# A list scheduler's model of two vector engines that take turns, new prices for products, and a reservation for the SSD transposes

## The chip, the cores and the metric

The kernel runs on one core of a Trainium2 chip. The metric is the device time of one execution in microseconds; the times of three runs and one profiled execution of the kernel before are given below.

## What is computed

Two layers of an encoder over 768 tokens (a prompt of 256 and a sample of 512, same weights, laid side by side). Cut to what matters:

```python
def _layer(x, ...):
    h = _rmsnorm(x, norm1_w)
    proj = h @ w_in                        # 1024 -> all mixer inputs and three gates
    o_ssd = _ssd_branch(z, xbc, dt_raw, ...)   # conv over 5 taps, silu, chunked scan both ways, 4 groups
    o_gla = _gla_branch(gq, gk, gv, gog, ...)  # gated linear attention, chunks of 64, both ways
    o_att = _attn_branch(aq, ak, av, ...)      # qk-norm, rotary, softmax
    merged = g0 * (o_ssd @ w_br_ssd) + g1 * (o_gla @ w_br_gla) + g2 * (o_att @ w_br_attn)
    x = x + merged @ w_out
    gate, up = _split(_rmsnorm(x, norm2_w) @ w_ffn_in, ...)
    return x + (silu(gate) * up) @ w_ffn_out
```

Everything is float32. Large products are made from operands split into a high and a low part of type float32r, with three products (high high, high low, low high) for each; small products inside the mixers are float32 or float32r.

## The kernel before, in words

Features lie on the partitions and the 768 tokens along the free dimension. A large product of 128 output features (`gemm_a`) is 24 or 48 matmuls of 384 columns into one of two PSUM tiles `g`. Each 128x512 unit of weights is loaded by SyncE, split by ScalarE (high part) and by GpSimd or VectorE (low part, `wunit`, L605): by GpSimd from the start of a layer to the end of the SSD, by VectorE after it.

A builder records every operation on views of named buffers, in program order. In a layer the order is: the projections for attention and for the other mixers with attention's own work between them (`att_group`); GLA, two pairs of heads (`gla_pair`), and then the eight products `g2`/`ba` (`gate_branch`); the SSD, where each of four groups has four products `xbc` with convolutions and transposes (`ssd_inputs`), the chunked scan of the group (`ssd_group`, `ssd_state`), and then one, three, two and two of the eight products `g1`/`bg`; then `z`, `g0`/`bs`, the output projection and the FFN.

`Plan.schedule` (L438) turns this into a fixed order for each engine's queue. It is a list schedule over a model: each engine takes, whenever it is idle in the model, the earliest operation in program order whose inputs are there and whose buffers are free (weights' splits and the evacuations of large products come first, `first`). What the model believes an operation to take comes from `Plan.cost` (L355): for VectorE 70 ns plus 1.04 ns per element (60 more with a scalar operand), for GpSimd's `tensor_tensor` 150 ns plus 2.1 ns per element, for a float32r product n / 2.4 ns. In the model every engine runs by itself. The program that is emitted holds the order alone; on the chip each engine goes through its queue and waits for what it needs.

Buffers are taken when the first operation that touches them is scheduled (`take`, L519). The tags of PSUM's `g` are taken in program order, so the large products follow each other in program order whatever the prices are; what the model sets is where the mixers' small products stand between them. PSUM has two tiles `ma` and two `mb` for small products, taken by whoever comes first. In the SSD the arrays `xn` (256 features by tokens) and `bn` exist once, and belong to one group at a time. The transposes of a group (L1411) write PSUM tiles `ma`, and ScalarE copies these into `xn` or `bn` (L1414). `reserve` (L382) lets one operation take further buffers together with its own; before the change attention alone uses it.

Of the kernel before, what the change touches and what calls it, by code (L numbers as in the profile page):

```python
# [16 lines left out]
P = 128  # L17
# [61 lines left out]
# gate inputs (16 columns each) that go with the products of 256 columns  # L79
# [5 lines left out]
# ---------------------------------------------------------------------------  # L85
# Recording and scheduling.  The builder below records engine operations on
# views of named buffers; `Plan` then orders them (a list schedule over the
# engines' queues) and emits them in that order into Tile, which derives every
# wait.  Buffers of phase 0 have their place for the whole program; the rest of
# SBUF is cut into cells, of which each holds, per phase, one Tile tile with  # L90
# buffers of one kind (operands of float32r products, or anything else).
# ---------------------------------------------------------------------------
class View:
# [82 lines left out]
    def region(self):  # L176
        """(first, last + 1) over partitions and over the elements of one."""
        dims = self.dims
        p = (0, 1)
        lo = hi = self.off[1]  # L180
        if self.buf.space in "SP":
            n, s = dims[0]
            p = (self.off[0], self.off[0] + (n - 1) * s + 1)
            dims = dims[1:]
        for n, s in dims:
            if s >= 0:
                hi += (n - 1) * s
            else:
                lo += (n - 1) * s
        hi += 1  # L190
        if self.buf.space == "P":
            lo, hi, p = lo // 512 * 512, -(-hi // 512) * 512, (0, 128)
        return p[0], p[1], lo, hi
# [62 lines left out]
class Op:  # L256
    __slots__ = ("i", "eng", "fn", "args", "kw", "deps", "succ", "cost", "prio", "bufs", "wait", "ready", "end",
                 "table", "label")
# [13 lines left out]
class Plan:  # L272
# [25 lines left out]
    def record(self, eng, fn, args, kw):  # L298
# [49 lines left out]
        op.cost = self.cost(eng, fn, writes[0], reads) + extra + 120 * ("accum_out" in kw)  # L348
        for j in deps:
            self.ops[j].succ.append(op)  # L350
# [4 lines left out]
    def cost(eng, fn, out, reads):  # L355
        n = out.free()
        if eng == "tensor":
            if fn == "transpose":
                return 107
            if out.buf.space == "P" and reads[0].dtype == F32R:  # L360
                return 3 + (n / 2.4 if n >= 256 else 4 * n / 2.4)
            return 3 + (210 if n <= 64 else 4 * n / 2.4)
# [18 lines left out]
    @staticmethod  # L381
    def reserve(op, *views):  # L382
        """The buffers of the views are taken together with those of the operation."""
        for b in {v.buf for v in views} - set(op.bufs):
            op.bufs.append(b)
            b.users += 1

# [36 lines left out]
    def home(self, slot):  # L424
        """The Tile tile that the buffers of a slot live in."""
# [12 lines left out]
    def schedule(self):  # L438
# [5 lines left out]
        self.dma_free = 0.0  # L444
# [16 lines left out]
        while ev:  # L461
# [11 lines left out]
            while todo:  # L473
# [3 lines left out]
                while avail[e]:  # L477
# [12 lines left out]
                    if e == "sync":  # L490
                        start = max(now, self.dma_free)
                        self.dma_free = start + cost
                        idle_at[e] = now + 60
                        op.end = start + cost + 1900
                    else:
                        op.end = idle_at[e] = now + cost
# [68 lines left out]
class Pool:  # L565
    """Tags of one phase: the buffers of later phases take the place of earlier ones."""
# [8 lines left out]
class Builder:  # L575
# [12 lines left out]
    def first(self):  # L588
        """What feeds the tensor engine's products goes before the mixers' operations."""
# [79 lines left out]
    def sumsq(self, src, accs, last, eng=None, which=0):  # L669
        """Squares of one tile of features, added up on a vector engine; the last tile is left to the product."""  # L670
# [12 lines left out]
    def rstd(self, accs, nat, pool=None, ts=(0, NT)):  # L683
        """1 / rms of each token: nat with the tokens on partitions, and as rows over all partitions."""
# [88 lines left out]
    def layer(self, l):  # L773
# [161 lines left out]
    def finish(self, ps, xa, acc):  # L935
        """The last tile of features, and the final norm, by halves of the tokens."""
# [30 lines left out]
    def gate_inputs(self):  # L967
        """The inputs of the gates (SSD steps, GLA low rank), features on partitions."""
# [140 lines left out]
    def att_heads(self, t, i, span, nk, j, qT, kT, v2, oh, ol):  # L1109
        """Two heads of one tile of queries; their output goes to the rows of one tile of features."""  # L1110
# [81 lines left out]
    def gla_pair(self, p):  # L1192
# [10 lines left out]
        for d in range(2):  # L1203
# [12 lines left out]
            # scores within blocks of 64  # L1216
# [13 lines left out]
            # between the blocks, and with the state  # L1230
# [158 lines left out]
    def ssd_inputs(self, g):  # L1389
# [4 lines left out]
        for i in range(4):  # L1394
# [12 lines left out]
            if i < 3:  # L1407
                for a, b in ((0, 3), (3, 6)):
                    pt = self.pm.tile([P, 512], F32, tag="ma")
                    for t in range(a, b):  # L1410
                        self.pe.transpose(pt[:, (t - a) * P:(t - a + 1) * P], acc[:, self.toff(t)], self.ident)  # L1411
# [12 lines left out]
    def three(self, o, lhs, rhs):  # L1424
        """A product of split operands: hi hi, hi lo and lo hi."""
# [202 lines left out]
```

## Time and profile before

| | us |
|---|---|
| three runs | 3242.95, 3247.67, 3248.82 |
| median | 3247.67 |
| span of the profiled execution, first to last instruction | 3241.8 |
| TensorE busy in it | 3076.5 (95%) |
| VectorE busy | 1830.7 (56%) |
| ScalarE busy | 1304.3 (40%) |
| GpSimd busy | 1053.0 (32%) |
| mean granted TensorE clock, share of 2.4 GHz | 0.983 |

The profiled execution is known by its span; no time is recorded for what lies around it, and the median of the runs is 5.9 us above the span. Busy time of TensorE counts the whole flight of a matmul, and matmuls are pipelined, so a busy TensorE is not one at its peak. Every operation is emitted from one line (L554), so the line tells nothing; forms of operands and the stretch of time do. `base_P` is PSUM, `base_S` the buffers that keep their place for the whole program, `cell` those that change from phase to phase.

### The profile page before, as it was taken

What the parts mean: (1) busy time and instruction counts of PE and PEld (TensorE: products, weight loads), DVE (VectorE), ACT (ScalarE), POOL (GpSimd) and SP (SyncE); (2) the same over time, 40 slices, a digit from 0 to 9 for tenths busy, and PEclk for the clock granted to TensorE, in tenths of its full rate; (3) what the DMA queues carried; (4) which work ended last, traced back from release to release, by engine and by line L of the source; (5) the groups of instructions that cost most, each with busy time, mean ns of one, the idle gap of its engine ahead of it and who ended that gap; (6) DMA issues with size and microseconds to landing.
All of it is one profiled execution on the core that took longest, in us unless ns stands there. A gap on an engine that the chain in (4) does not pass through costs nothing.

```text
span 3241.8 us, 47503 instructions
## 1 busy us (share of the span) xinstructions
PE 3076.5 (95%) x18288; PEld 3003.9 (93%) x18288; DVE 1830.7 (56%) x3115; ACT 1304.3 (40%) x2285; POOL 1053.0 (32%) x1028
## 2 busy tenths in 40 slices
PE   8989988888999999999999899889899999999998
PEld 8989888878999999999999898788889999999998
DVE  4866888888523332333458568898884234333233
ACT  4756655444423221212356665454443232222123
POOL 5524656565232000000164255565642320000002
PEclk8999999999999999999999999999999999999999
DMA  3123223443334322222322232333333352222222
GB/s 115 59 70 111 73 73 96 108 108 100 101 87 128 117 66 62 62 66 62 97 69 62 69 114 69 90 92 95 108 114 95 87 174 67 62 65 62 62 62 69
DMA packets 191954, 279.49 MB, mean 86 GB/s; under 512 B 16688, under 2 KB 89776, under 8 KB 191728
## 3 DMA queue, kind: packets, MB, share of 16 engines
q1 hardware_dynamic: 191728, 276.46, 29.1%
q8 instruction: 144, 2.36, 0.3%
q14 instruction: 82, 0.67, 0.1%
HBM read 235.30 MB, written 41.09 MB: 85 GB/s over the span
## 4 chain that ended last, share of the span: by engine, by line
PE 75%; DVE 18%; ACT 2%; issue 2%; DMA 2%; POOL 1%; DVEq 0%; SPq 0%; POOLq 0%; ACTq 0%
PE base_P L554 75%; DVE cell L554 16%; DVE base_S L554 2%; ACT cell L554 1%; POOL cell L554 1%; DMA cell<-d_cs 1%; DMA d_ce<-cell 1%; ACT base_S L554 0%; ACT L554 0%; DMA cell<-d_ce 0%; POOL base_S L554 0%; DMA cell<-xT 0%; SPq L554 0%; DVEq L1623 0%; DVEq L554 0%
## 5 line engine op out<-in xcount | busy, mean ns | idle before, releaser
L554 PE MATMUL base_P<-base_S 128*128 128x384 f32 (+3 forms) x12452 | 2290.7, 336 | 10.0 <-DVE base_S L554 5.9
L554 PEld LDWEIGHTS base_P<-base_S 128*128 128x128 f32 x12452 | 2118.3, 191 | 18.5 <-DVE base_S L554 7.5
L554 ACT ACTIVATE base_S<-base_S 128x512 fp32r<-128x512 f32 (+6 forms) x830 | 550.0, 667 | 1242.3 <-PE base_P L554 889.0
L554 POOL TENSOR_TENSOR cell<-cell,base_S 128x512 f32<-128x512 f32 (+3 forms) x308 | 338.7, 1115 | 1387.4 <-ACT base_S L554 1289.3
L554 DVE TENSOR_TENSOR base_S<-base_S,base_S 128x512 fp32r<-128x512 f32 (+1 forms) x400 | 283.6, 709 | 680.9 <-issue 516.3
L554 PE MATMUL base_P<-cell,base_S 128*128 128x384 f32 x3136 | 574.5, 337 | 0.0
L554 PEld LDWEIGHTS base_P<-cell,base_S 128*128 128x128 f32 x3136 | 551.0, 188 | 0.0
L554 POOL TENSOR_TENSOR base_S<-base_S,base_S 128x512 fp32r<-128x512 f32 (+1 forms) x232 | 331.3, 1429 | 342.3 <-ACT base_S L554 186.6
L554 PE MATMUL base_P<-cell,cell 128*128 128x256 f32 (+3 forms) x1696 | 335.4, 316 | 104.6 <-DVE cell L554 85.8
L554 PEld LDWEIGHTS base_P<-cell,cell 128*128 128x128 f32 x1696 | 257.6, 196 | 145.6 <-DVE cell L554 90.5
L554 DVE TENSOR_TENSOR base_S<-base_P,base_S 128x768 f32<-128x768 f32 x228 | 217.6, 954 | 224.9 <-PE base_P L554 217.9
L554 DVE SCALAR_TENSOR_TENSOR cell<-cell,base_S,cell 128x128 f32<-128x128 f32 (+1 forms) x320 | 263.7, 858 | 30.5 <-ACT cell L554 27.5
L554 DVE TENSOR_TENSOR cell<-base_P,cell 128x256 f32<-128x256 f32 (+6 forms) x401 | 196.1, 496 | 144.9 <-PE base_P L554 117.2
L554 ACT ACTIVATE cell<-cell 128x256 fp32r<-128x256 f32 (+7 forms) x362 | 191.3, 545 | 179.8 <-DVE cell L554 146.6
L554 DVE TENSOR_TENSOR cell<-cell,cell 128x256 fp32r<-128x256 f32 (+7 forms) x282 | 217.6, 791 | 16.7 <-ACT cell L554 9.8
L554 ACT ACTIVATE cell<-base_P 128x256 f32<-128x256 f32 (+6 forms) x344 | 147.7, 439 | 188.9 <-PE base_P L554 182.4
L554 ACT ACT_TABLE_LOAD x147 | 188.6, 1283 | 29.3 <-DVE cell L554 21.6
L554 PE MATMUL base_P<-base_S,cell 128*128 128x128 f32 (+2 forms) x908 | 154.8, 278 | 30.4 <-DVE cell L554 16.6
L554 POOL TENSOR_TENSOR cell<-cell,cell 128x256 f32<-128x256 f32 (+6 forms) x196 | 134.3, 702 | 113.1 <-DVE cell L554 84.0
L554 PEld LDWEIGHTS base_P<-base_S,cell 128*128 128x128 f32 x908 | 112.9, 149 | 49.6 <-DVE cell L554 22.0
L554 DVE SCALAR_TENSOR_TENSOR cell<-cell,base_S 128x128 f32<-128x128 f32 x192 | 114.3, 646 | 8.1 <-POOL cell L554 6.5
L554 POOL TENSOR_TENSOR base_S<-base_S 128x768 f32<-128x768 f32 x32 | 66.5, 2077 | 96.5 <-DVE base_S L554 96.1
(57 smaller groups left out, 1147.4 us busy)
## 6 DMA issues: line engine op xcount, KB each, us to landing
base_S<-wts SPq DMA_DIRECT2D x584, 256.0 KB, 2.7
cell<-d_cs SPq DMA_DIRECT2D x96, 256.0 KB, 4.6
d_part<-base_S SPq DMA_DIRECT2D x32, 384.0 KB, 2.6
base_S<-d_part SPq DMA_DIRECT2D x32, 384.0 KB, 3.3
base_S<-wts SPq DMA_DIRECT2D x32, 272.0 KB, 2.7
d_y<-cell SPq DMA_DIRECT2D x48, 128.0 KB, 1.9
base_S<-d_y SPq DMA_DIRECT2D x16, 384.0 KB, 3.4
d_x<-base_S SPq DMA_DIRECT2D x16, 384.0 KB, 2.5
```

The source lines that it names most:

```text
L554: f(*[real(x) for x in op.args], **{k: real(x) for k, x in op.kw.items()})
```

## The change

Three edits; the rest of the diff takes comments out.

First, an operation gets a flag `port`: set for every operation of GpSimd, and for those of VectorE whose operands all lie in SBUF. In the model a flagged operation starts only when the flagged one scheduled before it has ended, so that the two engines take turns. Second, the prices of products: a float32r product of 384 columns goes from 163 to 175.3 ns, float32 ones are priced by the same 0.4486 ns per column, small ones at 222 ns. Third, the first of each three SSD transposes takes `xn` or `bn` together with its PSUM tile. No operation is added or removed; the emitted program has the same operations, and their order and the place of some buffers come out anew.

```diff
+        op.port = eng == "gpsimd" or eng == "vector" and all(v.buf.space == "S" for v in writes + reads)
...
-                return 3 + (n / 2.4 if n >= 256 else 4 * n / 2.4)
-            return 3 + (210 if n <= 64 else 4 * n / 2.4)
+                return 3 + (.4486 * n if n >= 256 else 4 * .4486 * n)
+            return 3 + (222 if n <= 128 else 4 * .4486 * n)
...
-        self.dma_free = 0.0
+        self.dma_free = port_free = 0.0
...
+                    elif op.port:
+                        op.end = idle_at[e] = port_free = max(now, port_free) + cost
                     else:
                         op.end = idle_at[e] = now + cost
...
-                        self.pe.transpose(pt[:, (t - a) * P:(t - a + 1) * P], acc[:, self.toff(t)], self.ident)
+                        tr = self.pe.transpose(pt[:, (t - a) * P:(t - a + 1) * P], acc[:, self.toff(t)], self.ident)
+                        if t == a:
+                            self.plan.reserve(tr, xn if i < 2 else bn)
```

## Rows read from the trace of the kernel before

**Rows 1.** The page: busy us of each engine, share of the span, instructions.
```profile
PE 3076.5 (95%) x18288; PEld 3003.9 (93%) x18288; DVE 1830.7 (56%) x3115; ACT 1304.3 (40%) x2285; POOL 1053.0 (32%) x1028
```

**Rows 2.** Stretches, layer one: length; PE, PEld, DVE, ACT, POOL busy (instructions); PEclk, DMA, GB/s.
```profile
50.00:286.00 236.00, 222.12 (x1545) 214.89 (x1543) 163.71 (x425) 150.57 (x340) 99.70 (x132) 0.98 0.25 75
286.00:437.00 151.00, 140.96 (x805) 131.53 (x804) 117.81 (x238) 89.81 (x169) 92.55 (x104) 1.00 0.27 83
437.00:465.00 28.00, 24.98 (x149) 23.95 (x148) 26.00 (x30) 17.19 (x26) 18.16 (x12) 1.00 0.21 58
465.00:537.00 72.00, 62.20 (x352) 57.73 (x351) 65.59 (x108) 30.26 (x53) 44.02 (x44) 0.93 0.34 99
537.00:549.50 12.50, 11.09 (x67) 10.58 (x67) 9.75 (x16) 9.83 (x16) 8.02 (x7) 1.00 0.20 54
549.50:622.00 72.50, 61.16 (x351) 57.57 (x351) 61.57 (x101) 28.30 (x49) 47.15 (x45) 0.93 0.43 114
622.00:650.00 28.00, 28.00 (x169) 27.66 (x168) 20.98 (x25) 17.23 (x26) 14.06 (x12) 1.00 0.26 73
650.00:718.00 68.00, 56.20 (x334) 52.01 (x333) 58.98 (x98) 27.38 (x48) 44.25 (x45) 0.97 0.43 113
718.00:742.00 24.00, 23.90 (x145) 23.42 (x144) 20.59 (x27) 15.79 (x24) 14.22 (x11) 1.00 0.22 64
...
802.00:1600.00 798.00, 798.00 (x4581) 797.97 (x4581) 288.25 (x366) 213.02 (x307) 78.78 (x40) 1.00 0.29 84
```

**Rows 3.** The same view, layer two, the stretch of its four SSD groups.
```profile
2068.00:2402.00 334.00, 291.51 (x1715) 274.69 (x1714) 295.38 (x470) 154.09 (x257) 206.47 (x197) 0.96 0.35 102
```

**Rows 4.** Waits in 465 to 802 us: who for whom: us, times, longest.
```profile
PEld base_P L554 <- DVE cell L554: 46.8, 41, 3.2
PE base_P L554 <- DVE cell L554: 41.8, 43, 2.9
...
DVE cell L554 <- PE base_P L554: 19.4, 17, 3.8
...
DVE cell L554 <- ACT cell L554: 17.2, 12, 4.0
```

**Rows 5.** VectorE by form, 465 to 802 us: busy us, mean ns; idle before, releasers.
```profile
L554 DVE SCALAR_TENSOR_TENSOR cell<-cell,base_S 128x128 f32<-128x128 f32 x88 | 53.4, 657 | 1.8 <-POOL cell L554 1.8
L554 DVE SCALAR_TENSOR_TENSOR cell<-cell,base_S,cell 128x128 f32<-128x128 f32 x96 | 53.3, 609 | 0.0
```

**Rows 6.** VectorE by form, 506.9 to 507.9 us, a stretch without GpSimd work.
```profile
L554 DVE SCALAR_TENSOR_TENSOR cell<-cell,base_S,cell 128x128 f32<-128x128 f32 x4 | 1.1, 341 | 0.0
```

**Rows 7.** GpSimd by form, 465 to 802 us: the splits of weights.
```profile
L554 POOL TENSOR_TENSOR base_S<-base_S,base_S 128x512 fp32r<-128x512 f32 x43 | 61.6, 1433 | 66.9 <-issue 19.7 <-PE base_P L554 18.5 <-ACT base_S L554 14.2
```

**Rows 8.** GpSimd in order of time around 506.9 us: start, us, operation, idle before.
```profile
510.20 1.33 POOL L554 TENSOR_TENSOR base_S<-base_S,base_S 128x512 fp32r<-128x512 f32 x1 [4.20 <-PE base_P L554]
```

**Rows 9.** TensorE in order of time: between groups two and three, products xbc.
```profile
631.20 0.81 PE L554 MATMUL base_P<-base_S,cell 128*128 128x128 f32 x6
631.77 11.08 PE L554 MATMUL base_P<-base_S 128*128 128x384 f32 x62
```

**Rows 10.** TensorE in order of time: the end of group one (128-column rows are transposes).
```profile
523.61 0.82 PE L554 MATMUL base_P<-base_S,cell 128*128 128x128 f32 x6
...
531.06 1.10 PE L554 MATMUL base_P<-cell,cell 128*128 128x64 f32 x8 [1.67 <-DVE cell L554]
```

**Rows 11.** GpSimd in order of time, in GLA.
```profile
368.50 1.20 POOL L554 MEMSET cell<- 64x768 f32 x2
```

**Rows 12.** VectorE in order of time, same place.
```profile
368.64 0.95 DVE L554 TENSOR_TENSOR cell<-cell,cell 64x768 f32<-64x768 f32 x1
```

**Rows 13.** VectorE by form, 286 to 437 us: the form of rows 12.
```profile
L554 DVE TENSOR_TENSOR cell<-cell,cell 64x768 f32<-64x768 f32 x8 | 14.9, 1858 | 0.3 <-ACT cell L554 0.2
```

**Rows 14.** GpSimd by form, 286 to 437 us: fills with zero.
```profile
L554 POOL MEMSET cell<- 64x128 f32 x30 | 6.0, 199 | 9.2 <-PE base_P L554 8.2
L554 POOL MEMSET cell<- 64x768 f32 x6 | 4.4, 732 | 3.2 <-PE base_P L554 3.1
```

More of the change, by code (lines that the diff above doesn't have):

```diff
@@ L257 @@
     __slots__ = ("i", "eng", "fn", "args", "kw", "deps", "succ", "cost", "prio", "bufs", "wait", "ready", "end",
-                 "table", "label")
+                 "table", "label", "port")
 class Proxy:
```

## The prediction

> **What bounds the kernel now.** First the page's busy times: TensorE 95%, VectorE 56%, GpSimd 32% [rows 1]. That share averages stages with different limits, so the second view is the table of stretches [rows 2]. From 802 to 1600 us (z, gates, output projection, FFN) TensorE is busy for all 798.00 us, with 4581 matmuls, 0.174 us each. Nothing that the change orders anew can shorten that half of a layer; VectorE has 288 us of work in it. The time in play is the mixers' part, from 50 to 802 us, and its copy in layer two.
>
> There the reader is to see that two limits alternate in the SSD. While a group's scan runs (465 to 537, 549.5 to 622, 650 to 718) TensorE is busy 62.20 of 72.00, 61.16 of 72.50 and 56.20 of 68.00 us, and VectorE 65.59, 61.57 and 58.98 us: VectorE is near its end and TensorE waits. Between the groups it is the other way round: from 622 to 650 TensorE is busy 28.00 of 28.00 us, from 718 to 742 it is 23.90 of 24.00, while VectorE has 20.98 and 20.59 and GpSimd 14.06 and 14.22 us [rows 2]. What TensorE does there is products xbc of the next group back to back, as the 62 matmuls of 384 columns in one run show [rows 9]. From group one to group two the gap is 12.50 us instead of 28 and 24 [rows 2]: only one gate product stands in the order after group one, so xbc of group two was run beside the scan. The waits say the same [rows 4]: from 465 to 802 us TensorE and its weight loads wait 41.8 and 46.8 us for VectorE, and VectorE in turn waits 19.4 us for TensorE and 17.2 for ScalarE. Layer two repeats it: VectorE 295.38 of 334 us [rows 3].
>
> Third, why VectorE is so full. A fused operation on 128x128 takes 657 and 609 ns in the mean in these groups [rows 5], and 341 ns where GpSimd rests [rows 6, 8]. The planner books 263 ns for it (70 + 1.04 x 128 + 60, in the code). For these 184 operations it books 48.4 us and the trace has 106.7. The two engines hold each other up, and the planner of before knows nothing of it: its picture is a scan that ends early and a TensorE that is the limit.
>
> **The change part by part.** No operation comes or goes, so no busy time of its own changes. What can move is waiting, and which of VectorE's operations meet one of GpSimd's.
>
> *Turns.* With the new flag a scan is as long in the book as on the chip, roughly. Its small products come ready later in the book, so TensorE's queue gets gate products and then xbc of the next group in front of them, during the scan, where it now waits 41.8 and 46.8 us [rows 4]. The large products keep their own order. Upper bound: the gaps of 28 and 24 us become 12.5 like the first, 15.5 + 11.5 = 27.0 us a layer. Lower bound for this step: nothing, because the work that VectorE does in the gaps does not vanish. If a gap shrinks to 12.5 us, VectorE's 20.98 and 20.59 us of it become 9.75, and 11.2 + 10.8 = 22.0 us go into the scans. VectorE's free time in those two scans is 72.50 - 61.57 and 68.00 - 58.98, 10.9 + 9.0 = 19.9 us, and part of that is spent waiting for ScalarE, which the order doesn't cure. Hiding half of the 22.0 gives 27.0 - 11.0 = 16 us; I take the middle of the bounds, 13 us a layer. It is two thirds of the 19.4 us that VectorE waits for TensorE [rows 4], which is the part of VectorE's idleness that a better order can take away. Two layers: 26 us.
>
> The 28 us from 437 to 465 are a gap as well, between GLA and the first scan; there VectorE is busy 26.00 of them and TensorE 24.98, so an earlier xbc would find VectorE full. I book nothing for it, between 0 and 15.5 us a layer (down to 12.5 like the others).
>
> *Prices of products.* 163 becomes 175.3 ns; the chip gives 174 [rows 2]. The mean price was 7% low. Where TensorE is the limit (802 to 1600) the queues of the others have so much room that nothing follows: 0. In the mixers it works against the first edit: a dearer large product lets the book put fewer of them between two small ones. It is one number in the same plan and can't be told apart; its bounds are in those above.
>
> *Reservation.* In group one the six transposes for group two run at 523.61 us, 7 us ahead of the last products that read the old `xn` at 531.06 [rows 10]. They hold both tiles `ma` from there until `xn` is free. With the reservation they come after, and the tiles stay with the scan. This is worth at most those 7 us a layer and costs at most the transposes' own 0.82 us and the copy behind them; for group three they run at 631.20 us, after the scan, anyway [rows 9]. I book 0, cover being the products xbc that TensorE has there; without that cover it would cost 0.8 us a layer.
>
> *Attention and GLA.* From 50 to 286 us TensorE is busy 222.12 of 236 us, from 286 to 437 us 140.96 of 151 [rows 2]. Some of the idle 14 and 10 us may be won or as much lost by a new order, and nothing in the rows says which: 0, bounds half of that idle time, 12 us a layer, either way.
>
> *A rule.* In GLA a 64x768 product on VectorE took 0.95 us beside two fills of GpSimd [rows 11, 12], where its mean is 1858 ns [rows 13]: fills do not hold VectorE up. The change books them as turns. The Trainium skill, page "SBUF — State Buffer", section "Who interferes with whom", says that a VectorE instruction with two SBUF inputs contends with a GpSimd instruction that reads SBUF and not with one that only writes it; the trace agrees (0.95 against 1858 ns). The sum by that rule is a rival below.
>
> **Sum.** 3241.8 - 2 x 13 = 3215.8 us of span; the median stands 5.9 us above the span, so 3221.7: **3222 us**. Its own range is from 27.0 us a layer (3194) to 3 us a layer (3241).
>
> **The rivals.**
>
> *More than that.* The scans have room, the moved work fits in, and the gap before the first scan shrinks too: 27.0 + 15.5 = 42.5 us a layer, 3248 - 85 = 3163 us; with the two later gaps alone 3194. For it: TensorE waits 88 us a layer in this part. Against it: VectorE at 85 to 91% in the scans.
>
> *No change, the turns are the limit.* If VectorE and GpSimd between them already use up a scan, what leaves the gap comes back in the scan one for one: 3248, give or take 6. For it: VectorE's 295.38 of 334 us [rows 3], and 43 splits of weights at 1433 ns that GpSimd has to fit between [rows 7]. Against it: half of VectorE's time on the 184 fused operations is waiting, and the gaps have room for turns.
>
> *Fills booked as turns.* The fills in GLA are 6.0 + 4.4 us a layer [rows 14]. If the book's GLA is longer by these and its products go behind as much of large ones, 10.4 us a layer come back: -26 + 21 = -5, 3243 us, no change.
>
> *Slower: small products behind large ones.* TensorE takes its queue in order. If the new book is late about the small products, these stand behind runs of large ones, and VectorE, the fuller engine, waits. Place: the four scans. By the code a group has 34 small steps with 138 of the 352 matmuls of the first scan [rows 2] (float32 ones appear twice in the trace); the other 214 make runs of 6, 1.1 us by 0.174 us each. Half a run, 0.55 us, for three steps on the path (state, product with the state, transposes) of 24 tiles is 40 us a layer, where VectorE now waits 19.4 [rows 4]: 20 more, 40 in two layers, less the 26 won: +14, 3262 us; with all four steps of a tile 3289. It decides from 13 us a layer on, that is, when VectorE's wait for TensorE in the SSD goes beyond some 32 us. For it: the book still has GpSimd's operations whole in the turn, and takes the worst of each meeting. Against it: the book is now close to the chip's own length.
>
> *It does nothing.* The model may order as before; with every price in the mixers changed this is next to impossible.
>
> **How the numbers follow.** Forecast 0.41; more than that 0.15; no change because of the turns 0.11; fills 0.05; slower 0.27, of which a little is lost in attention and GLA; the rest 0.01. About 0.2% (6.5 us) is what a measurement of this kernel tells from no change: faster by over 0.2% 0.57, within 0.16, slower 0.27. The range takes in most of "more" and most of "slower": 3170 to 3276. The likeliest case alone is 3194 to 3241.
>
> **What would show it.** Right: in the table of stretches the gaps between groups go to some 12 us with TensorE no longer at 100%, the scans are longer than now by less than the gaps are shorter, TensorE's 41.8 and 46.8 us of waits fall, and VectorE's 19.4 us with them; the transposes stand after the last products of the group before. Wrong by turns: gaps shorter, scans longer by as much. Wrong by the slower rival: VectorE's wait for TensorE in the SSD above 32 us. From 802 to 1600 us nothing should move; if it does, my reading of what the change reaches is wrong.

## The result and the profile after

The changed kernel takes 3338.1 us (median of four runs, 3334.6 to 3340.6) where the kernel before takes 3247.9: 1.0283 times as long, 95% interval 1.0271 to 1.0296. The forecast of 3222 us was wrong in sign, and 3338 lies above the range of 3170 to 3276 too. The profiled execution's span went from 3241.8 to 3337.8 us, 96 us more.

Below, "before" and "after" are the two kernels, "the book" is the timetable that the planner reckons with, a "gap" is the stretch between the scans of two SSD groups, the "taps" are the 16 operations on 128x770 with which VectorE makes the convolutions of one group, and an "evacuation" is the operation that empties a PSUM tile of a large product. The page's busy line of after, which answers [rows 1]:

```profile
PE 3149.7 (94%) x18288; PEld 3058.7 (92%) x18288; DVE 1807.3 (54%) x3115; ACT 1307.4 (39%) x2279; POOL 1028.6 (31%) x1028
```

VectorE and GpSimd are each some 24 us less busy than before, TensorE 73 us more with the same instructions. The table of stretches of after, layer one, with the columns of [rows 2]. In order: start to the end of attention, GLA, the gap ahead of the SSD, then scan, gap, scan, gap, scan, gap, scan, and the rest of the layer; the last row is the SSD of layer two [rows 3].

```profile
50.00:309.00 259.00, 238.85 (x1597) 226.11 (x1596) 164.29 (x426) 156.02 (x348) 101.77 (x132) 0.95 0.27 69
...
312.00:491.00 179.00, 159.90 (x854) 145.43 (x855) 123.88 (x253) 94.48 (x174) 94.93 (x104) 0.92 0.24 73
...
491.00:513.00 22.00, 21.61 (x130) 21.21 (x129) 16.84 (x17) 15.79 (x23) 16.69 (x12) 1.00 0.20 54
513.00:573.50 60.50, 45.59 (x211) 39.41 (x210) 50.15 (x96) 17.60 (x37) 34.53 (x38) 0.69 0.35 97
573.50:600.00 26.50, 26.50 (x151) 26.38 (x151) 20.81 (x26) 16.75 (x25) 11.45 (x10) 0.94 0.18 49
600.00:676.00 76.00, 67.45 (x399) 65.50 (x398) 62.79 (x101) 29.17 (x51) 49.20 (x50) 0.91 0.46 127
676.00:702.00 26.00, 26.00 (x150) 25.90 (x149) 20.27 (x26) 16.30 (x24) 10.69 (x10) 0.94 0.17 47
702.00:771.00 69.00, 59.83 (x328) 56.21 (x328) 56.33 (x99) 26.71 (x48) 43.46 (x46) 0.83 0.42 116
771.00:796.00 25.00, 25.00 (x151) 24.90 (x150) 20.66 (x26) 16.63 (x25) 11.02 (x10) 1.00 0.18 49
796.00:864.00 68.00, 59.05 (x331) 56.02 (x330) 56.37 (x105) 27.69 (x48) 31.30 (x36) 0.85 0.39 104
...
864.00:1650.00 786.00, 785.01 (x4508) 784.69 (x4507) 285.68 (x357) 207.51 (x300) 78.44 (x40) 1.00 0.28 83
...
2160.00:2509.00 349.00, 308.38 (x1706) 293.42 (x1705) 287.27 (x473) 150.52 (x250) 191.05 (x193) 0.85 0.34 98
```

The reader is to see three things. The stretch up to the end of attention is 23 us longer (259 against 236), with VectorE's work the same, 164.29 against 163.71 us. GLA is 28 us longer (179 against 151). And the gaps between the SSD groups, 12.5, 28 and 24 us before, are 26.5, 26 and 25: two did not shrink, and the short one has grown to the length of the others. The second half of the layer is as full as before.

A sum over the whole trace says the same. For each product I took the time from its start to the start of the next, less the usual time for its form (the median in the kernel before), and put what is over on the stage of the product that waited, the second of the two. It is worked out from the order-of-time view and the plan's order, both layers together; two runs that come below stand beside:

| TensorE time lost, us | attention | GLA and g2 | SSD and g1 | rest | sum |
|---|---|---|---|---|---|
| before | 67 | 62 | 160 | 22 | 311 |
| after | 88 | 98 | 182 | 32 | 400 |
| after less before | 21 | 36 | 22 | 10 | 88 |
| e2, new prices without turns | 80 | 63 | 188 | 24 | 356 |
| e17, turns in attention alone | 80 | 79 | 193 | 28 | 381 |

88 of the 96 us are there, the largest part in GLA. The sum is firm and its split less so: put on the product before the wait, GLA's part is 42 us and that of the rest nothing.

### The profile page after: what moved, and what is told of

The parts are those of the page before. It is cut to its first block, busy times and chain, and to the rows that moved or that the text cites. A ratio compares the mean times of both kernels' runs of the same rounds, so it can differ in the third digit from the quotient of the medians.

```text
span 3337.8 us, 47472 instructions
## 1 busy us (share of the span) xinstructions
PE 3149.7 (94%) x18288; PEld 3058.7 (92%) x18288; DVE 1807.3 (54%) x3115; ACT 1307.4 (39%) x2279; POOL 1028.6 (31%) x1028
## 5 line engine op out<-in xcount | busy, mean ns | idle before, releaser
L557 PE MATMUL base_P<-base_S 128*128 128x384 f32 (+3 forms) x12452 | 2252.4, 335 | 15.5 <-DVE base_S L557 11.0
L557 POOL TENSOR_TENSOR cell<-cell,base_S 128x256 f32<-128x256 f32 (+3 forms) x308 | 328.4, 1079 | 1381.9 <-ACT base_S L557 1272.2
L557 PE MATMUL base_P<-cell,cell 128*128 128x256 f32 (+3 forms) x1696 | 383.3, 357 | 139.6 <-DVE cell L557 97.6
L557 PEld LDWEIGHTS base_P<-cell,cell 128*128 128x128 f32 x1696 | 293.5, 227 | 188.8 <-DVE cell L557 100.1
L557 POOL TENSOR_TENSOR base_S<-base_S,base_S 128x512 fp32r<-128x512 f32 (+1 forms) x232 | 315.1, 1361 | 339.8 <-ACT base_S L557 157.2
L557 DVE SCALAR_TENSOR_TENSOR cell<-cell,base_S,cell 128x128 f32<-128x128 f32 (+1 forms) x320 | 256.0, 834 | 17.1 <-ACT cell L557 14.2
L557 ACT ACTIVATE cell<-cell 128x256 fp32r<-128x256 f32 (+8 forms) x362 | 190.5, 545 | 127.4 <-DVE cell L557 115.6
L557 DVE TENSOR_TENSOR cell<-cell,cell 128x256 fp32r<-128x256 f32 (+6 forms) x278 | 204.6, 752 | 13.4 <-ACT cell L557 8.3
L557 PE MATMUL base_P<-base_S,cell 128*128 128x128 f32 (+2 forms) x908 | 170.5, 297 | 16.8 <-DVE cell L557 13.2
L557 DVE SCALAR_TENSOR_TENSOR cell<-cell,base_S 128x128 f32<-128x128 f32 x192 | 99.8, 550 | 8.4 <-POOL cell L557 5.2
```

The costliest lines, as they stand in the source:

```text
L557: f(*[real(x) for x in op.args], **{k: real(x) for k, x in op.kw.items()})
```

## The experiments

"Prices" are those of products, "turns" the flag `port`. Each kernel is a changed kernel with the edit shown unless it says otherwise. Times are medians, ratios are to the kernel before.

**The three edits one by one.** `e1_reserve` has the reservation alone, `e2_prices_reserve` the prices too, `e3_turns_reserve` the reservation and the turns:

```diff
-        op.port = eng == "gpsimd" or eng == "vector" and all(...)
+        op.port = False                                      # e1, e2
-                return 3 + (.4486 * n if n >= 256 else 4 * .4486 * n)
+                return 3 + (n / 2.4 if n >= 256 else 4 * n / 2.4)   # e1, e3; the line below likewise
```

> The kernel before with the reservation alone; old prices, no turns. Theory T (turns: the book puts the mixers' small products behind large ones, and the end of each mixer stands bare): no change, 3248 us within 7. Theory R (the reservation itself costs, because the transposes of a group now wait for the group before): most of the 90 us, 3310 to 3340. Theory P (dearer products): 3248.

> The changed kernel without the turns; new prices and reservation. Theory T: the loss is gone, 3230 to 3262 us. Theory P (with products dearer by 7% the book lets fewer of them run between small ones): 3300 or more. Theory R: as the run with the reservation alone.

> The changed kernel with the old prices of products; turns and reservation. Theory T: the loss stays, 3315 to 3365 us. Theory P: 3250 to 3270. Theory R: as the run with the reservation alone.

Measured: e1 3249.3 us (ratio 0.9999, 0.9988 to 1.0010), e2 3288.3 (1.0134, 1.0104 to 1.0163), e3 3381.4 (1.0421, 1.0390 to 1.0451). With after as the fourth corner:

| us, all with the reservation | old prices | new prices |
|---|---|---|
| no turns | 3249 | 3288 |
| turns | 3381 | 3338 |

The reservation costs nothing. Two values lie outside what was expected: e2 between the two theories' ranges, e3 above all of them. The two other edits don't add up: the dearer products cost 39 us without turns and win 43 with them, the turns cost 132 us with the old prices and 50 with the new. So neither edit has a worth of its own; it depends on how dear the other kind of work is in the book. Since the plan with turns comes to no end without the reservation (transposes hold both `ma` tiles and wait for `xn`), that corner was not run.

**The price.** `e10_price_of_384` is e2 with the old prices for float32 products, so that the dearer column of float32r products (163 to 175.3 ns for the large ones, and the mixers' products of 256 columns in proportion) is alone.

> Reservation, no turns, and of the new prices that of float32r products alone (163 to 175.3 ns for 384 columns); the small products at the old ones. Theory B (dearer large products let the small ones run ahead, the gaps between SSD groups get longer): 3275 to 3300 us, the gaps as in the run with all prices. If the prices of small products make the 40 us: 3240 to 3260.

3281.2 us (1.0108, 1.0070 to 1.0145): of the 39 us, some 32 are this one number (its two runs lie 10 us apart, 3276.4 and 3286.0), and it is the one that was made true to the chip's 174 ns. The gaps of e2, from group one to group four, show where it goes:

```profile
538.00:560.00 22.00, 19.95 (x115) 19.33 (x113) 16.94 (x20) 13.40 (x22) 11.77 (x9) 0.95 0.20 54
...
627.00:667.00 40.00, 39.58 (x227) 39.04 (x227) 19.64 (x26) 17.67 (x27) 18.57 (x15) 0.97 0.32 88
...
733.00:761.00 28.00, 27.84 (x160) 27.45 (x160) 18.45 (x24) 16.83 (x25) 14.25 (x12) 0.96 0.21 62
```

The gaps are 22, 40 and 28 us, 26 more than the 64.5 before [rows 2]: 502 matmuls stand in them, against 381, so products that ran beside a scan before now stand in the gap.

**Where the turns cost.** `e6_turns_in_ssd`, `e17_turns_in_attention` and `e18_turns_in_gla` have turns in one stage of each layer alone; the builder numbers its stages, 2 to 7 for the first layer and 8 to 12 for the second:

```diff
+        op.port = (...) and self.phases in (5, 10)        # e6; (2, 3, 8) in e17, (4, 9) in e18
```

> The changed kernel with turns in the SSD's operations alone; new prices and reservation everywhere. Against the run with prices and reservation (3288 us; gaps between its SSD groups of 22, 40 and 28 us in layer one). By the step of the prediction the gaps fall to some 12 us and the time to 3255 to 3275. By theory S (in the SSD the turns move the gaps, not the sum; the loss of the changed kernel is made in attention and GLA): 3280 to 3300. If the SSD's turns carry the loss: 3315 or more.

> New prices and the reservation, turns only for operations from a layer's start to the end of attention. By e2 3288 us without turns, by the changed kernel 3338 with all, by e6 17 us won with those of the SSD: the turns of attention and GLA cost some 67 us together. If attention's are the cause (its products held back, GLA left without large products beside it), most of it is here: 3325 to 3355. If it is GLA's own turns, it stays at 3285 to 3305.

> New prices and the reservation, turns only for operations in the stretch of GLA. If attention's turns are the cause, within 15 us of e2: 3275 to 3303. If GLA's own are, 3325 to 3355. If both count and add up, e17 and e18 lie above 3288 by 67 us together.

Against e2's 3288.3: e6 3271.6 us, 17 less (1.0076, 1.0047 to 1.0105); e17 3319.6, 31 more (1.0215, 1.0175 to 1.0256); e18 3292.7, 4 more (1.0132, 1.0103 to 1.0162). So attention's turns are the costly ones, though by less than the 37 us that I had set for it, and those of the SSD help. One by one they sum to 18 us, not to the 50 of after. For the other 32 there is no run: none has two stages with turns, and none has those from z to the FFN alone. By the table above after loses 8 us more in attention and 18 more in GLA than e17, so GLA's turns are the likely partner of attention's.

e6 is in the range of the prediction's step, 3255 to 3275 us, and its gaps are not the 12 us that the step gave for it. They are as long as after's:

```profile
537.00:563.50 26.50, 26.50 (x156) 26.39 (x155) 21.46 (x28) 16.97 (x25) 11.37 (x11) 0.96 0.21 52
...
638.50:665.00 26.50, 26.50 (x152) 26.39 (x151) 21.17 (x27) 16.45 (x24) 11.10 (x10) 0.94 0.20 51
...
734.00:761.00 27.00, 27.00 (x156) 26.90 (x155) 21.51 (x28) 17.00 (x25) 11.40 (x11) 0.94 0.19 51
```

The stretches of attention and GLA, first in e17, then in e18:

```profile
50.00:303.00 253.00, 234.48 (x1595) 221.08 (x1594) 164.51 (x426) 155.40 (x347) 101.72 (x132) 0.97 0.28 71
307.00:476.00 169.00, 154.48 (x851) 141.37 (x851) 126.75 (x248) 93.11 (x173) 94.59 (x104) 0.98 0.26 78
```
```profile
50.00:278.00 228.00, 210.22 (x1447) 197.19 (x1446) 157.43 (x420) 142.71 (x329) 95.98 (x128) 0.97 0.24 69
282.00:465.00 183.00, 171.26 (x968) 161.65 (x968) 125.55 (x254) 102.30 (x183) 99.86 (x108) 0.98 0.27 80
```

e17 ends attention at 303 us (before 283, e2 276), and by then the products g2, which should run beside GLA, have been running since 251 (before, from 260 to 283). In e18 GLA is longer than in e17, 183 against 169 us, but TensorE is at work in it, 171.26 us, and little is lost: a longer stage need not cost where large products stand beside it. By the sum used above GLA loses 79 us in e17, 61 in e18 and 98 in after, against 63 in e2; attention itself loses no more in e17 than in e2.

**What in the turns costs.** `e8_fills_free` takes GpSimd's fills out of the turns, `e9_scalars_free` VectorE's results of up to 8 elements per partition, and `e4_turns_that_contend` leaves only GpSimd's operations other than fills and VectorE's with two inputs of more than 8 elements, all in SBUF:

```diff
+        op.port = eng == "gpsimd" and fn != "memset" or ...              # e8
+        op.port = eng == "gpsimd" or eng == "vector" and writes[0].free() > 8 and all(...)   # e9
+        op.port = (eng == "gpsimd" and fn != "memset") or (eng == "vector" and
+            len([v for v in reads if v.free() > 8]) > 1 and all(...))    # e4
```

> The changed kernel with GpSimd's fills taken out of the turns, nothing else. Turns for those that contend alone gave 3275 us, 63 under the changed kernel. If the fills make that: 3270 to 3295. If the one-input operations of VectorE (attention's reductions and scalings) make it: 3320 to 3345.

> The changed kernel with VectorE's operations on a few scalars per partition (results of up to 8 elements: attention's maxima, reciprocals, sums) taken out of the turns, nothing else. Theory A (each of attention's heads has some of these in its chain, and in the book each waits for a split of weights of 1225 ns; the book holds attention back, its products go behind large ones, and GLA after it stands bare): 3265 to 3300 us, attention's last product 25 to 40 us earlier in layer one. If the larger one-input operations make it (the scaling of 512 probabilities, the copies in GLA): 3320 to 3345.

> The changed kernel with turns only for those that hold each other up: GpSimd's operations but its fills, and VectorE's with two SBUF inputs. If the over-billed turns (fills, one-input operations) make the loss, most of it goes: 3250 to 3285 us. If the turns as such make it (theory T), it stays within a third: 3305 to 3345.

e8 3339.1 us (1.0284, 1.0254 to 1.0313), e9 3295.8 (1.0153, 1.0123 to 1.0182), e4 3274.9 (1.0093, 1.0063 to 1.0122), against after's 3338.1: the fills are worth nothing, the tiny operations 42 us, all operations that don't contend 63. All but a handful of the tiny ones are attention's, 114 a layer: the scaling of the row maxima, the reciprocals, the sums of squares of the norms of q and k. (The maxima themselves read PSUM and take no turn.) VectorE by form in after, up to the end of attention, and below it the same form before:

```profile
L557 DVE RECIPROCAL cell<-cell 128x1 f32<-128x1 f32 x48 | 7.7, 161 | 31.4 <-ACT cell L557 30.7
```
```profile
L554 DVE RECIPROCAL cell<-cell 128x1 f32<-128x1 f32 x48 | 7.7, 161 | 19.5 <-ACT cell L554 19.1
```

161 ns in both; of the 96 in the whole of after, 30 lie wholly inside an operation of GpSimd with two inputs and take 158 ns in the mean. In the book such an operation can wait for a split of weights, for which the code books 1225 ns (150 + 2.1 x 512). Running the planner of after shows that 37 of the 114 wait at all, for 23 us together in a layer; how these grow into the 42 us, through a softmax that comes late in every queue, is argued and not shown. Freed of that, attention of e9 is as long as before, 236 us, and 479 products of g2 are left to run beside GLA, against 442 in after and 482 before:

```profile
50.00:286.00 236.00, 222.98 (x1556) 214.71 (x1555) 166.29 (x425) 150.58 (x343) 99.25 (x130) 0.98 0.26 74
```

The Trainium skill, page "SBUF — State Buffer", section "Who interferes with whom", draws the same line for these operations: a VectorE instruction with at most one SBUF input does not contend with GpSimd, outside VectorE's 2-port modes. The trace agrees for the tiny ones (158 ns beside GpSimd, 161 in the mean); no run here tells of the operations that the page lets enter those modes. What it costs to book all these as turns is 63 us, e4 against after.

**What makes an SSD gap.** My working took a gap for a run of large products. `e13_evacuations_first` puts two evacuations of each product xbc ahead of VectorE's other work, so that xbc runs beside the scan:

```diff
+            with self.first():
                 self.dve.tensor_tensor(out=raw[:, 2:2 + TA], in0=ps[:, 0:TA], ...)
                 self.dve.tensor_tensor(out=raw[:, TA + 4:T + 4], in0=ps[:, TA:T], ...)
```

> The changed kernel with one thing more: the two evacuations of each product xbc into its raw buffer come ahead of VectorE's other work in the book, as the evacuations of other large products do. In the changed kernel's queue 92 products xbc and 41 gate products stand in each gap between two SSD groups; here no xbc stands there any more, the next group's run beside the scan, and 103 to 117 gate products have come in their place. If the xbc that are stuck behind VectorE make the gaps (the working of the prediction), the gaps of 27, 26 and 25 us go to some 12 and the time falls by 2 x 3 x 13 us, to some 3260. If a gap is as long as the chain of convolutions, transposes and first steps of the scan, which stands after the scan of the group before in either order, the gaps stay within 3 us of 27, 26, 25 and the time stays within 15 us of 3338.

3352.9 us (1.0322, 1.0292 to 1.0352), as the second theory had it. The gaps of e13, and VectorE's 128x770 operations (the taps of the convolutions, 16 per group) in the first:

```profile
581.00:610.00 29.00, 24.93 (x136) 24.13 (x136) 25.25 (x31) 19.80 (x27) 11.24 (x7) 0.87 0.21 63
...
684.00:713.00 29.00, 25.10 (x138) 24.49 (x139) 25.31 (x31) 20.18 (x27) 11.57 (x7) 0.88 0.22 61
...
780.00:806.00 26.00, 21.94 (x121) 21.28 (x121) 22.94 (x31) 19.44 (x26) 7.72 (x5) 0.87 0.15 44
```
```profile
L557 DVE SCALAR_TENSOR_TENSOR cell<-cell,base_S,cell 128x770 f32<-128x770 f32 x14 | 18.8, 1340 | 2.3 <-ACT cell L557 2.0
```

With xbc gone the gaps are 29, 29 and 26 us. Large products still stand in them, gate products g1 in place of xbc (117, 119 and 102 of 384 columns, against 133 in each gap of after), but they no longer fill them: TensorE idles 4.1 us in each, and waits for VectorE all that time. So not the products xbc make a gap as long as it is; the best candidate is the work of VectorE, the convolutions of the next group that have not been done beside the scan. Counted in each gap by the view by form:

| kernel | gaps, us | taps in them |
|---|---|---|
| before | 12.5, 28, 24 | 5, 12, 10 |
| e2 | 22, 40, 28 | 9, 12, 12 |
| after | 26.5, 26, 25 | 13, 13, 13 |
| e13 | 29, 29, 26 | 14, 14, 13 |
| e14 | 18, 20, 18 | 8, 10, 8 |
| e11 | 12, 18, 14 | 6, 9, 9 |

But for one a gap is 1.6 to 2.5 us per tap. That is no proof by itself, since a longer stretch takes in more of everything, and VectorE is not the limit at every moment: in e2's second gap it waits 12.2 us for TensorE, and in the first gap of after, where TensorE never idles, 3.36 us for a product xbc:

```profile
582.49 1.02 DVE L557 TENSOR_TENSOR cell<-base_P,base_S 128x256 f32<-128x256 f32 x2 [3.36 <-PE base_P L557]
```

Why the taps are late: in the changed kernel's book VectorE, with its waits for the turn, is taken up for practically all of the first scan's 34 us, and about half of that is waiting; it takes the earliest operation in program order, so the next group's evacuations and taps come after the scan. Both PSUM tiles `g` then stay full, and TensorE runs out of large products beside the scan; the book has the same hole, 44 us long. In after no product of 384 columns stands between these two rows of TensorE, 40 us apart:

```profile
530.20 0.69 PE L557 MATMUL base_P<-base_S 128*128 128x384 f32 x3
...
571.43 1.63 PE L557 MATMUL base_P<-base_S 128*128 128x384 f32 x4
```

**Is it that an engine stands still in its turn?** `e14_other_work_in_turn` is after, and `e15_contending_other_work` e4, with the step that an engine takes other work while it waits for its turn:

```diff
+                    if op.port and port_free > now:
+                        later.append(op)
+                        continue
...
+                offer(later)
```

> The changed kernel with one thing more: where the turn is the other engine's, VectorE or GpSimd takes the next operation that needs no turn, instead of standing still until its turn has come. The set of operations with turns, the prices and the reservation are those of the changed kernel. If the turns lose time because an engine that waits for one stands still in the book (VectorE for 16 us of the 34 us of its first scan), so that evacuations and one-input operations come too late in the queues, most of the 90 us come back: under 3280. If it is the turns of operations that do not contend on the chip (the tiny ones cost 42 us, e9), whether the engine stands still or not, it stays above 3310. In the queue the gaps hold 97, 74 and 97 large products instead of 133.

> e4 (turns only for GpSimd's operations other than fills and VectorE's with two SBUF inputs of more than 8 elements) with the step of e14. If standing still is what is left of the loss (e4 3275 against 3248 before), this falls below 3248; if what is left is the dearer products, whose loss e2 showed by itself (3288), it stays between 3260 and 3280.

e14 3333.1 us (1.0261, 1.0231 to 1.0291), e15 3299.9 (1.0159, 1.0129 to 1.0188; e4 without the step is 3274.9). It is not the standing still: e14 stays where the other theory had it, above 3310, and e15 lies above what either gave. The gaps of e14 did shrink, and the scans grew by more; scan, gap, scan, gap, scan, gap of e14:

```profile
503.00:599.00 96.00, 86.86 (x512) 82.60 (x513) 64.08 (x112) 42.02 (x67) 57.64 (x56) 0.98 0.37 109
599.00:617.00 18.00, 16.88 (x98) 16.19 (x97) 16.01 (x19) 14.13 (x20) 9.99 (x8) 1.00 0.39 110
617.00:702.00 85.00, 77.09 (x459) 73.14 (x459) 64.19 (x107) 34.20 (x59) 52.86 (x51) 0.98 0.39 104
702.00:722.00 20.00, 15.06 (x78) 14.65 (x77) 15.85 (x21) 13.12 (x18) 7.25 (x6) 0.83 0.17 46
722.00:798.00 76.00, 69.48 (x421) 65.08 (x421) 63.03 (x111) 36.44 (x60) 44.34 (x42) 1.00 0.42 116
798.00:816.00 18.00, 17.54 (x107) 17.18 (x105) 15.48 (x24) 16.50 (x23) 6.11 (x5) 1.00 0.35 97
```

Three gaps are 22 us shorter than after's and three scans 51 us longer. That is not a loss of 29 us, since the whole of e14 is 5 us shorter than after: the three scans hold 1392 matmuls against 938, 454 more, which at 0.174 us each are 79 us of products moved in. TensorE is still only 90 to 91% busy in them. Shorter gaps came with longer scans and brought the total next to nothing, which is the outcome that the rival "no change, the turns are the limit" had named.

**Keeping TensorE's clock up.** `e5_kept_warm` is after with dummy products wherever the book has TensorE idle ahead of a small product.

```diff
+                        for _ in range(min(int(gap / 230), 12) if o is not None else 0):
+                            self.nc.tensor.matmul(real(o[:, :w]), lhsT=real(self.warm), ...)
```

> The changed kernel's order, with small idle products (ones by ones, 128 columns, into the PSUM tile that the next small product overwrites) put on TensorE where the book has it idle; they add work and no result. Theory C (a part of the 90 us is that TensorE, idle in the bare ends, is granted 1.2 GHz and then takes twice as long for the small products on the path): granted clock from 0.948 to over 0.97 and the time down by 15 to 45 us, 3295 to 3325. If the waits alone make the loss: the clock rises and the time stays or grows, 3335 to 3365.

3373.4 us (1.0389, 1.0359 to 1.0419). The cores' view of e5, of after and of before, and GLA in e5:

```profile
core 0: 3370.7 us, clock 0.985
```
```profile
core 0: 3337.8 us, clock 0.948
```
```profile
core 0: 3241.8 us, clock 0.983
```
```profile
314.00:492.00 178.00, 165.44 (x971) 154.45 (x970) 119.65 (x239) 93.89 (x175) 95.55 (x108) 0.98 0.25 74
```

The time is above what either theory gave, the clock is back at before's, and GLA is 178 us long with a clock of 0.98, as it was 179 in after with 0.92. So the clock's return did not bring the time back. But e5 does not separate the clock from the waits: its dummies are 1576 further records on TensorE, some 175 us at the usual 112 ns, while the time lost, by the sum above, falls from 400 to 263 us. What they fill and what they hold up can't be told apart. What the lower clock costs in after stays open; an estimate of the most that it can be, from the order-of-time view, is 52 us of the 88: 797 products of after start at the lower level and 310 before, and if each lost by it what it lost in all, but no more than its usual time, that is 87 us against 35.

**Other balances.** `e7_engines_dearer` has no turns and instead every price of VectorE and GpSimd times 1.2. `e11_mixed` has e4's turns in attention and GLA, and in the SSD no turns but prices times 1.2; `e12_old_prices_contend` has e4's turns in attention and GLA with the old prices; `e16_mixed_evacuations_first` is e11 with the step of e13.

```diff
+        op.cost *= 1.2 if eng in ("vector", "gpsimd") else 1                       # e7
+        op.port = (contending) and self.phases in (2, 3, 4, 8, 9)                  # e11, e12, e16
+        if self.phases in (5, 10) and eng in ("vector", "gpsimd"): op.cost *= 1.2  # e11, e16
```

> New prices of products and reservation, no turns, but every operation of VectorE and GpSimd booked at 1.2 times its price. Theory B (what counts is how dear the mixers' operations are in the book against the products: prices alone let the small products run ahead of too few large ones, full turns put them behind too many): a value between the two, near the kernel before, 3235 to 3265 us. If dearer products lose for another reason: 3280 or more.

> New prices and reservation; turns for those that contend in attention and GLA only; in the SSD no turns, VectorE and GpSimd at 1.2 times their price. By the lost TensorE time of the runs so far, stage by stage (attention 59, GLA 39, SSD 157, the rest 40 us in two layers), 295 us, as much as the kernel before (297): 3230 to 3262. If a stage's loss depends on the stage ahead of it, not on its own book: 3265 or more.

> Old prices and reservation; turns for those that contend in attention and GLA only, none in the SSD. If turns that are true to the chip help where nothing else is changed: 3225 to 3243 us. If the old, optimistic book was already at the better balance and every turn moves it off: 3255 to 3300.

> e11 (3234 us) with the evacuations of xbc ahead, as in e13. The queue of TensorE changes little by it (192, 138 and 134 products xbc in the scans instead of 192, 128 and 146). If VectorE's lateness with the evacuations is a limit in this order too, 5 to 15 us less than e11; if the orders differ only by chance, within 10 us of it, either way.

e7 3269.6 us (1.0074, 1.0051 to 1.0096), between its two ranges: a plain factor wins as much against e2 as e6's turns. e11 3234.0 us (0.9953, 0.9934 to 0.9972), the only one faster than before, by half a per cent; e12 3309.7 (1.0196, 1.0166 to 1.0225), above both of its ranges; e16 3248.0 (0.9999, 0.9988 to 1.0010). The gaps of e11:

```profile
550.00:562.00 12.00, 12.00 (x76) 11.92 (x75) 10.69 (x14) 9.81 (x16) 5.62 (x6) 1.00 0.24 67
...
641.00:659.00 18.00, 18.00 (x109) 17.94 (x108) 15.28 (x18) 13.57 (x20) 12.91 (x10) 1.00 0.22 56
...
733.00:747.00 14.00, 14.00 (x84) 13.41 (x82) 13.82 (x17) 8.82 (x16) 6.57 (x7) 1.00 0.35 100
```

Here the taps are done beside the scans, and 12, 18 and 14 us is what the forecast hoped for: the SSD loses 142 us against 160 before, by the sum used above. But e16, for which neither theory had more than 10 us of loss, changes one right of way and is 14 us slower, so e11 is one good order, not a rule for prices. It also means that a new order alone can be worth some 14 us here: differences of that size between two of these kernels, e6's 17 us and e18's 4 among them, need not have the cause that the edit suggests.

## The prediction, step by step

The sum gave 26 us won; 90 were lost, 39 with the new prices (e1 to e2) and 50 with the turns (e2 to after). The steps that failed are the two that were put at nothing, the prices and the turns' effect in attention and GLA, and the picture of a gap behind the third.

**Turns, 13 us a layer won.** This step failed in its picture of a gap. I read TensorE's 28.00 of 28.00 busy us [rows 2] and the 62 matmuls in one run [rows 9] as TensorE being what a gap waits for. They say only that large products were there to fill it. VectorE, whose 20.98 and 20.59 us in those gaps I had in hand and counted as work to be moved, has to finish the taps before the gap can end; e13 took the products xbc out and the gap stayed. The second error was in the direction: I had the turns put the small products late, behind more large ones. They also make VectorE late with the evacuations that the large ones wait for, and the first scan of after lost its large products for 40 us. With new prices and turns in the SSD alone the kernel gains 17 us over e2 (e6), of 26 booked. That the size is near is luck: the gaps of e6 are 26.5, 26.5 and 27 us and none is 12; what shrank is e2's longest, of 40 us, which the kernel before does not have.

**What VectorE gains from turns.** The meetings did become rarer. VectorE by form from 513 to 863 us of after, answering [rows 5], and GpSimd's splits, answering [rows 7]:

```profile
L557 DVE SCALAR_TENSOR_TENSOR cell<-cell,base_S,cell 128x128 f32<-128x128 f32 x96 | 50.2, 577 | 0.0
L557 DVE SCALAR_TENSOR_TENSOR cell<-cell,base_S 128x128 f32<-128x128 f32 x88 | 46.6, 557 | 2.9 <-POOL cell L557 2.9
```
```profile
L557 POOL TENSOR_TENSOR base_S<-base_S,base_S 128x512 fp32r<-128x512 f32 x41 | 55.0, 1342 | 76.1 <-PE base_P L557 27.5 <-ACT base_S L557 26.9 <-ACT cell L557 18.8
```

577 and 557 ns instead of 609 and 657: 10 us a layer, of the 44 that separate the 184 operations from 341 ns each [rows 6]. The program fixes an order on each engine and not between two, so operations that take turns in the book still meet on the chip.

**Prices, 0.** Mis-sized: 39 us without turns (e2), some 32 of them the large product's. The mechanism was in the text, "it works against the first edit", but I took it as bounded by the other term because the two "can't be told apart". They could (e2, e3), and the price has either sign, 39 us lost without turns and 43 won with them.

**Reservation, 0.** Right: 3249.3 us. The 0.8 us a layer without cover would be too little to see.

**Attention and GLA, 0 with 12 us a layer either way.** Mis-sized, and the largest miss: by the sum above 10 us a layer are lost in attention and 18 in GLA, 28 together, where nothing was booked. Of attention's, 7 come with the new prices (e2). Of GLA's, 8 come with attention's turns alone (e17) and none with GLA's alone (e18); the rest needs several stages with turns. The bound was half of the idle time that there was, 14 and 10 us. That bounds a gain; nothing bounds a loss by the idle time of before.

**The rival "more"** had a count in its favour that is none. Its 88 us a layer of waiting add the waits of TensorE's products to those of its weight loads, which are in large part the same waits: by [rows 2] TensorE is idle for 34.5 of the 277 us from 465 to 742.

**The rival "fills booked as turns"** had its rule right and the wrong operations: fills are worth nothing (e8), the tiny one-input operations that the same rule spares are worth 42 us (e9).

**The rival "slower"** had the sign, and half of its mark. Waits of after from 513 to 863 us, answering [rows 4]:

```profile
PEld base_P L557 <- DVE cell L557: 42.6, 35, 3.3
...
PE base_P L557 <- DVE cell L557: 34.3, 31, 3.1
DVE cell L557 <- PE base_P L557: 30.7, 27, 3.5
...
DVE base_S L557 <- PE base_P L557: 11.9, 13, 2.2
```

VectorE's wait for TensorE with work in `cell` went from 19.4 to 30.7 us; with that in `base_S`, 1.5 and 11.9 us, from 20.9 to 42.6. That lies on both sides of the 32 us that were to decide, by which of the two is counted. But its place, the SSD, holds only 22 of the 88 us; its price, 14 us, was far too small because nothing in it spoke of attention and GLA.

**The second half of the layer unchanged.** Right: 785.01 of 786.00 us busy.

What stays open: why all turns together cost 32 us more than those of the three stages one by one, how much of the loss is the lower clock of TensorE, the 10 us in the rest of the layer, and why e12 with less in turns is better than e3 and still worse than e1.

## What to carry to other kernels

A list scheduler's book is a balance between prices: making one of them truer (163 to 175 ns, against a chip at 174) cost 1% here, so test each price alone and both together before they are taken as one edit. A stretch in which an engine is 100% busy does not say that this engine sets its length; count what the other engines must finish before the stretch can end, here most likely the taps. And a model of contention should hold only the operations that contend: here the exclusive turn for those that don't cost 63 us.

## What had not been expected of the chip

The granted clock stood at 0.50, the lower level of 1.2 GHz, from 545 to 571 us of after, a stretch in which TensorE had run only small products since 531 with waits of up to 3 us between them:

```profile
545.00:571.40 26.40, 17.71 (x66) 14.25 (x67) 22.71 (x51) 6.78 (x14) 14.08 (x17) 0.50 0.33 84
```

Before, the lowest scan of layer one stood at 0.93 [rows 2]. The mean of one small product of 64 columns, over the whole execution, was 288 ns before; in after it is 363 and in e5 279, in this order:

```profile
L554 PE MATMUL base_P<-cell,cell 128*128 128x64 f32 x384 | 55.4, 288 | 25.5 <-DVE cell L554 25.3
```
```profile
L557 PE MATMUL base_P<-cell,cell 128*128 128x64 f32 x384 | 75.7, 363 | 40.5 <-DVE cell L557 39.3 <-ACT cell L557 0.9
```
```profile
L568 PE MATMUL base_P<-cell,cell 128*128 128x64 f32 x384 | 51.6, 279 | 0.0
```

In after 224 of the 384 start at the lower level, before 39; from the start of one to the start of the next they take 213 ns there, in the median, and 112 at the upper one. So TensorE's 73 us of added busy time are in good part small products at the lower clock, 20 us in this form alone. Whether the time would come back with the clock, if nothing else were added, no run shows.
